# A hybrid decoder step on one core: the pooling copies go from ScalarE to VectorE, the last group's additions from GpSimd to VectorE, and the samples' last products are written later

## The chip, the cores and the metric

The kernel runs on one core of a Trainium2 chip. The metric is the device time of one execution in microseconds (us). A core has TensorE (matrix products, in the profile PE, with its weight loads as PEld), VectorE (DVE), ScalarE (ACT), GpSimd (POOL) and SyncE (SP), which here only issues transfers. Each engine works through its own queue in order.

## The reference

One layer of a decoder, for a prompt of 1024 rows and for 8 samples of 8 rows with their own states. All is float32.

```
h = rmsnorm(x) * (1 + scale) + shift                 # shift, scale, gate from silu(c) @ w_ada + b_ada
u_pool, z_pool, z_ssm, xBC, dt, g = split(h @ w_in)
P = (pool_mix(u_pool) * silu(z_pool)) @ w_pool_out   # pool_mix: means over 2, 4, 8, 16 rows, minus u,
                                                     # times pool_w (128x128 a group), times pool_scale
S = rmsnorm((SSD(silu(conv(xBC))) + D*x) * silu(z_ssm)) @ w_ssm_out
x = x + gate * ((sigmoid(g_pool) * P + sigmoid(g_ssm) * S) @ w_o)
y = rmsnorm(x)
```

It also returns the new states: the last 15 inputs of the pooling branch, the last 3 rows of the convolution's input, and the SSD state.

## The kernel before

Channels lie on the 128 partitions and the 1088 rows (1024 of the prompt, then 64 of the samples) along the free axis, up to the last product. Every large product is made of three TensorE products in a split format: each operand is halved into a high and a low part (`split`, L165 on ScalarE for the high part, L168 on GpSimd for the low one), and high x high, high x low and low x high are added in one PSUM bank. PSUM is handed out in pools: three banks named mm, four named ps, one named pc. Who asks for a bank waits until what was in it has been read.

The stages follow one another. First the norm and the modulation. Then `h @ w_in`, two blocks of 128 columns at a time, by a scheme of seven half-size products for eight (`pair`, `strassen`, `product`, L608 to L610); VectorE gathers the sums (L619, L624). Each pair's two column blocks have a generator for what happens to them afterwards: `u_unit` and `zp_unit` for the pooling branch (four pairs, with the windows 16, 8, 4 and 2 in this order), `conv_unit` for the convolution. Their steps are handed out between the products of later pairs (`between`, `step`). The last step of `u_unit`, the pooling tail, is what the first edit is about: the last 15 prompt rows and the sample rows of the group are turned by TensorE into one PSUM bank (L804, L805), copied out (L807, L808) and stored (L809, L810); then the means are multiplied by pool_w in three blocks of 256, 384 and 448 columns (L814), each copied out times pool_scale (L815). `zp_unit` multiplies that by silu(z) on VectorE (L828) and stores it.

Then comes the SSD in 4 groups of 8 chunks, with the products by w_pool_out (first) and w_ssm_out (three of the four groups of channels) woven in (L359 to L361, evicted by L1744). The fourth, last group stands by itself: for each of the 8 output tiles m, `tail_unit(m)` runs 36 products in three blocks, each added to the tile `acc[m]` from PSUM by VectorE (L1907); when the third is in, the tile is multiplied by the gate over the norm (L1912; the gate tile R is loaded by L1897 and scaled by L1900) and the pooling part m1 is added (L1913; loaded by L1902). For m = 0 to 6 the addition is GpSimd's, for m = 7, which goes in three blocks, VectorE's. Then `m_split` halves the tile for the last product: L1880 and L1881 for the samples' 64 columns, L1891 and L1892 for the prompt's 1024. Gate tiles have three buffers, so that the load for m + 3 waits for L1912 of m.

The last product, by w_o, turns the layout: for each of 8 blocks of 128 rows, two halves of 512 columns are summed over k = 0 to 7 (L2004 to L2006), times the gate (L2007), plus x, norm, store. The samples' rows have two sums of their own, over the same k, in a ps and the pc bank (`samples[k]`, L1886). Rows k = 0 to 4 of w_o (halves made earlier, loaded by `wo_prep`, L1873 and L1874) come early; rows 5 to 7 go to the buffers of the last group's inputs and can be loaded only when TensorE has read these. The function `sample_rows` finishes the samples between the blocks (L1968 and following).

SP's queue issues nearly all loads, in order; ScalarE's queue issues the stores. The order of the instructions on each engine isn't all written out by hand: the scheduler reorders within the traced program by a model of durations and by priorities, so an edit can shift instructions of other lines. In the SSD part TensorE and SP are held to the written order (`in_line`).

Of the kernel before, what the change touches and what calls it, by code (L numbers as in the profile page):

```python
# [10 lines left out]
AF = mybir.ActivationFunctionType  # L11
ALU = mybir.AluOpType
# [8 lines left out]
P = 128  # L21
# [4 lines left out]
NS = 64  # L26
# [20 lines left out]
def tile_pool_ssd_step(  # L47
# [6 lines left out]
    nc = tc.nc  # L54
    uid = [0]

    def nm(s):
        uid[0] += 1
        return f"{s}_{uid[0]}"
# [31 lines left out]
    def R(shape=(P, T), dt=F32):  # L91
        return hs.tile(list(shape), dt, tag="R", name=nm("R"), bufs=3)
# [4 lines left out]
    def PB():  # L97
        return psB.tile([P, 512], F32, tag="ps", name=nm("ps"))
# [14 lines left out]
    act = nc.scalar.activation  # L113
    V = nc.vector
# [31 lines left out]
    pscl = vT[:, 40:44]  # L146
# [601 lines left out]
    def GA(shape):  # L748
        return gas[0].tile(list(shape), F32, tag="GA", name=nm("GA"), bufs=7)

    def small(shape, tag, bufs):
        return gas[0].tile(list(shape), F32, tag=tag, name=nm(tag), bufs=bufs)
# [3 lines left out]
    def u_unit(gi):  # L756
        L = gi + 1
        stp = sm.tile([120, P], F32, tag="stc", name=nm("stp"), bufs=4)
        load(stp, state_pool[0, :, :, gi * P:(gi + 1) * P].rearrange("b t c -> (b t) c"))
        pwt = sm.tile([P, P], F32, tag="stc", name=nm("pwt"), bufs=4)  # L760
        load(pwt, pool_w[0, gi])
        yield
        up = GA([P, CW_])
        us = small([P, NB, 23], "us", 1)

        def done(o, n, comb, buf):
            e = min(o + n, SEQ) - o
            comb(up[:, 15 + o:15 + o + e], 0, e)
            if e < n:
                comb(us[:, :, 15:23], e, n, lambda t: t.rearrange("p (b t) -> p b t", t=8))  # L770
        yield done
        V.memset(up[:, 0:15], 0.0)
        ps = PB()
        nc.tensor.transpose(ps[:, :120], stp, ident[:120, :120])
        V.tensor_copy(us[:, :, 0:15], ps[:, :120].rearrange("p (b t) -> p b t", t=15))
        u64 = sm.tile([P, NB, 8], F32, tag="rsm", name=nm("u64"))
        act(u64, us[:, :, 15:23], AF.Copy)
        u15 = sm.tile([P, 27], F32, tag="t27", name=nm("u15"))
        act(u15[:, 0:15], up[:, SEQ:SEQ + 15], AF.Copy)
        yield  # L780
        a, av = up, us
        ab = [GA([P, T]) for _ in range(2)]
        for l in range(L):
            st = 1 << l
            o0 = 2 * st - 1
            b = ab[l % 2]
            bv = small([P, NB, 23], "bv", 2)
            V.tensor_tensor(b[:, o0:15 + SEQ], a[:, o0:15 + SEQ], a[:, o0 - st:15 + SEQ - st], ALU.add)
            V.tensor_tensor(bv[:, :, o0:], av[:, :, o0:], av[:, :, o0 - st:23 - st], ALU.add)
            a, av = b, bv  # L790
            if l or L < 4:
                yield 1
        wn = WINS[gi]
        d = ab[L % 2]
        V.scalar_tensor_tensor(d[:, :SEQ], a[:, 15:15 + SEQ], 1.0 / wn, up[:, 15:15 + SEQ], ALU.mult, ALU.subtract)
        e = sm.tile([P, 15], F32, tag="edge", name=nm("edge"), bufs=1)
        V.tensor_tensor(e[:, :wn - 1], a[:, 15:15 + wn - 1], rc[:, :wn - 1], ALU.mult)
        V.tensor_tensor(d[:, :wn - 1], e[:, :wn - 1], up[:, 15:15 + wn - 1], ALU.subtract)
        V.scalar_tensor_tensor(d[:, SEQ:].rearrange("p (b t) -> p b t", t=8), av[:, :, 15:], 1.0 / wn,
                               us[:, :, 15:], ALU.mult, ALU.subtract)  # L800
        yield 1
        yield 1
        ps = PB()
        nc.tensor.transpose(ps[:15, :P], u15[:, 0:15], ident)  # L804
        nc.tensor.transpose(ps[:NS, P:2 * P], u64.rearrange("p b t -> p (b t)"), ident)  # L805
        o15, o64 = [sm.tile([n, P], F32, tag="o27", name=nm("o15")) for n in (15, NS)]
        act(o15, ps[:15, :P], AF.Copy)  # L807
        act(o64, ps[:NS, P:2 * P], AF.Copy)  # L808
        store_(new_pool_p[0, 0, :, gi * P:(gi + 1) * P], o15)  # L809
        store_(new_pool_s[0, :, 7:15, gi * P:(gi + 1) * P], o64)  # L810
        y = up[:, :T]
        for o, n in BLK:
            ps = PB()
            mm(ps[:, :n], pwt, d[:, o:o + n], start=True, stop=True)  # L814
            act(y[:, o:o + n], ps[:, :n], AF.Copy, scale=pscl[:, gi:gi + 1])  # L815
        yp_[gi] = y
        yield 1

# [622 lines left out]
    def upair(gi):  # L1441
        return pair(C_UP + gi * P, C_ZP + gi * P, u_unit(gi), zp_unit(gi))
# [398 lines left out]
    def M(shape=(P, T), dt=F32):  # L1841
        return mq.tile(list(shape), dt, tag="m", name=nm("m"))
# [6 lines left out]
    ps = PB()  # L1849
    for c in range(9):  # L1850
        n = min(P, T - c * P)
# [5 lines left out]
    for c in range(9):  # L1857
        n = min(P, T - c * P)
# [7 lines left out]
    samples = []  # L1866

    def wo_prep(k, mem):
        if k < 4:
            hi, lo = w4[0][:, k, :D], w4[1][:, k, :D]  # L1870
        else:
            hi, lo = mem((P, D), F32R), mem((P, D), F32R)
        load(hi.bitcast(F32), wo_d[k][:, 0])  # L1873
        load(lo.bitcast(F32), wo_d[k][:, 1])  # L1874
        wo[k] = (hi, lo)

    def m_split(k, mem):

        sh = sm.tile([P, P], F32R, tag="stc", name=nm("sh"), bufs=4)
        act(sh[:, 0:NS], acc[k][:, SEQ:], AF.Copy)  # L1880
        V.tensor_tensor(sh[:, NS:P], acc[k][:, SEQ:], sh[:, 0:NS].bitcast(F32), ALU.subtract)  # L1881

        def sample_mm():
            for part in wo[k]:
                for half in range(2):
                    mm(pso[half], sh, part[:, half * 512:half * 512 + 512],  # L1886
                       start=(k == 0 and part is wo[k][0]), stop=(k == 7 and part is wo[k][1]))
        samples.append(sample_mm)
        hi, lo = mem((P, SEQ), F32R), mem((P, SEQ), F32R)
        for o, n in (((0, 384), (384, 384), (768, 256)) if k == 7 else ((0, SEQ),)):  # L1890
            act(hi[:, o:o + n], acc[k][:, o:o + n], AF.Copy)  # L1891
            V.tensor_tensor(lo[:, o:o + n], acc[k][:, o:o + n], hi[:, o:o + n].bitcast(F32), ALU.subtract)  # L1892
        mh[k], ml[k] = hi, lo

    def m_done(m):
        r = R()
        load(r, gs_d[m])  # L1897
        for j, ps in enumerate(rstd):
            s = slice(512 * j, min(512 * j + 512, T))
            V.tensor_tensor(r[:, s], ps[:, :s.stop - s.start], r[:, s], ALU.mult)  # L1900
        mt = M()
        load(mt, m1_d[m])  # L1902
        a = acc[m]

        def done(o, n, ps):
            s = slice(o, o + n)
            V.tensor_tensor(a[:, s], ps[:, :n], a[:, s], ALU.add)  # L1907
            if m < 7:
                s = slice(0, T)
                if o + n < T:  # L1910
                    return
            V.tensor_tensor(a[:, s], a[:, s], r[:, s], ALU.mult)  # L1912
            (nc.gpsimd if m < 7 else V).tensor_tensor(a[:, s], a[:, s], mt[:, s], ALU.add)  # L1913
        return done

    def tail_unit(m):
# [16 lines left out]

    def late(shape, dt=F32R):
        return slots.pop(0)[:, :shape[1]]
    for k in (5, 6):
        wo_prep(k, late)
        samples[k]()
    wo_prep(7, late)
    m_split(7, late)  # L1940
    sample_mm = samples[7]

    def w2k(tag):
        return wp.tile([P, 512], F32, tag=tag, name=nm("half"), bufs=4)
# [16 lines left out]
        nc.gpsimd.tensor_tensor(selS[:, pr], ident[:, 0:64], ident[:, 64:128], ALU.add)  # L1961

    def sample_rows():
        sample_mm()
        qs = []
        for half in range(2):
            q = w2k("wlo")
            act(q, pso[half], AF.Copy)  # L1968
            qs.append(q)
        yield  # L1970
        pq = PB()
        for half in range(2):
            mm(pq[64 * half:64 * half + 64, :], selS[:, 64 * half:64 * half + 64], qs[half], start=True, stop=True)
        V.tensor_tensor(gsm, pq, gsm, ALU.mult)
        V.tensor_tensor(gsm, gsm, xs_, ALU.add)
        act(xs_, gsm, AF.Square, accum_out=sso[:, 8:9])
        yield
        ps = PB()
        mm(ps[:, 0:1], selS, sso[:, 8:9], start=True, stop=True)
        act(sso[:, 8:9], ps[:, 0:1], AF.Sqrt, bias=eps, scale=1.0 / D)  # L1980
        V.reciprocal(sso[:, 8:9], sso[:, 8:9])
        V.scalar_tensor_tensor(gsm, gsm, sso[:, 8:9], fgs, ALU.mult, ALU.mult)
        for half in range(2):
            store_(ysr[:, half * 512:half * 512 + 512], gsm[64 * half:64 * half + 64])

    sample = sample_rows()
    for i in range(8):
        if i > 0:
# [10 lines left out]
        for j, (c0, cw) in enumerate(cuts):  # L1999
            s = slice(c0, c0 + cw)  # L2000
            ps = PB()
# [56 lines left out]
```

## Time and profile before

| | us |
|---|---|
| median of 3 runs | 1286.67 (1284.23 to 1289.22) |
| profiled execution, its own time | 1286.55 |
| its span in the profile | 1284.8 |
| TensorE busy | 1256.1 |
| VectorE busy | 897.6 |
| ScalarE busy | 662.2 |
| GpSimd busy | 670.9 |

The granted clock of TensorE was 0.998 of full speed on average. In a row of the waits view stand who waited for whom, the us in total, how often, and the longest. In a row of the timeline stand the start from the beginning of the span, the duration, engine, line, operation, tiles and shape, and in brackets how long the engine was idle before and what released it. PE durations are modelled and overlap: consecutive matmuls are told apart by their starts. "SPq" and "ACTq" are instructions of a queue that issue a transfer.

### The profile page before, as it was taken

Reading aid. Unit: us, or ns where it says so; the run is one execution under the profiler, and the core shown is the slowest. Engines: PE = TensorE matmul, PEld = TensorE weight load, DVE = VectorE, ACT = ScalarE, POOL = GpSimd, SP = SyncE. Lnnn points to the kernel's source line nnn. Section 1 sums busy time; section 2 is a strip of 40 time slices with the busy share of each in tenths; the row PEclk is TensorE's granted clock in tenths of the full one; section 3 lists DMA queues with packets and bytes.
Section 4 is the critical chain, followed back from the end, with each engine's and each line's share of the span. In section 5 each row is a group of like instructions: output and inputs, shape, how many; then the busy total and the mean of one; then the engine's idle time right before and its main releaser. Section 6 shows DMA issues by size and latency. Waiting matters only on the chain.

```text
span 1284.8 us, 26305 instructions
## 1 busy us (share of the span) xinstructions
PE 1256.1 (98%) x9739; PEld 1169.3 (91%) x9739; DVE 897.6 (70%) x1608; ACT 662.2 (52%) x1528; POOL 670.9 (52%) x563
## 2 busy tenths in 40 slices
PE   7999999999999999999999999999999999999997
PEld 6779999989999999999999999989888889999786
DVE  4686678965978688676676765587766877576443
ACT  4665347465556556454655554656675766202111
POOL 1007669678868878555444444355665867314000
PEclk9999999999999999999999999999999999999999
DMA  9736355465456544444556564999769898675631
GB/s 331 243 118 215 122 164 156 149 199 173 148 161 207 159 152 131 166 154 122 176 170 198 165 191 143 336 307 314 225 215 277 265 294 265 211 265 162 229 107 49
DMA packets 232769, 251.68 MB, mean 196 GB/s; under 512 B 29729, under 2 KB 176881, under 8 KB 232634
## 3 DMA queue, kind: packets, MB, share of 16 engines
q1 hardware_dynamic: 160544, 171.60, 42.9%
q10 hardware_dynamic: 72098, 78.41, 17.9%
q8 instruction: 77, 1.26, 0.4%
q14 instruction: 50, 0.41, 0.1%
HBM read 167.06 MB, written 83.01 MB: 195 GB/s over the span
## 4 chain that ended last, share of the span: by engine, by line
PE 63%; issue 7%; DMA 7%; POOL 4%; ACT 2%; DVE 2%; SPq 0%; ACTq 0%; POOLq 0%; DVEq 0%
PE ps L608 6%; PE ps L609 5%; PE ps L610 5%; PE mm L608 5%; PE mm L610 5%; PE mm L609 5%; PE mm L359 4%; PE mm L360 4%; PE mm L361 4%; PE ps L1213 3%; PE ps L2004 2%; PE ps L2006 2%; PE ps L2005 2%; PE pc L1535 2%; PE ps L1216 2%
## 5 line engine op out<-in xcount | busy, mean ns | idle before, releaser
L168 POOL TENSOR_TENSOR wlo<-rawA,whi 128x512 fp32r<-128x512 f32 x120 | 179.6, 1501 | 176.1 <-ACT whi L165 99.8
L168 POOL TENSOR_TENSOR wlo<-raw,whi 128x512 fp32r<-128x512 f32 x92 | 150.6, 1644 | 125.5 <-ACT whi L165 114.1
L359 PE MATMUL mm<-Y,whi 128*128 128x352 f32 (+1 forms) x480 | 163.5, 341 | 0.6 <-DVE G L1907 0.5
L360 PE MATMUL mm<-Y,whi 128*128 128x352 f32 (+1 forms) x480 | 157.4, 328 | 0.3 <-DVE Y L1573 0.3
L361 PE MATMUL mm<-Y,wlo 128*128 128x352 f32 (+1 forms) x480 | 156.8, 327 | 0.0
L608 PE MATMUL mm<-Y,whi 128*128 128x272 f32 x496 | 146.3, 295 | 0.6 <-DVE GA L624 0.5
L610 PE MATMUL mm<-Y,wlo 128*128 128x272 f32 x496 | 144.2, 291 | 2.2 <-POOL wlo L168 1.7
L608 PE MATMUL ps<-Y,whi 128*128 128x272 f32 x496 | 143.4, 289 | 2.5 <-ACT o L808 2.2
L609 PE MATMUL ps<-Y,whi 128*128 128x272 f32 x496 | 143.0, 288 | 0.0
L610 PE MATMUL ps<-Y,wlo 128*128 128x272 f32 x496 | 142.6, 287 | 0.0
L609 PE MATMUL mm<-Y,whi 128*128 128x272 f32 x496 | 142.6, 288 | 0.0
L1056 DVE SCALAR_TENSOR_TENSOR GA<-GA,cvT,GA 128x1112 f32<-128x1112 f32 x72 | 127.7, 1776 | 1.3 <-ACT GA L1053 1.3
L165 ACT ACTIVATE whi<-rawA 128x512 fp32r<-128x512 f32 x125 | 78.3, 627 | 89.7 <-PE ps L609 48.0
L165 ACT ACTIVATE whi<-raw 128x512 fp32r<-128x512 f32 x96 | 58.9, 627 | 104.6 <-DVE raw L554 48.7
L1201 ACT ACTIVATE dec<-dec,acT 128x128 f32<-128x128 f32 (+1 forms) x288 | 86.6, 383 | 23.2 <-POOL dec L1192 22.8
L610 PEld LDWEIGHTS mm<-Y,wlo 128*128 128x128 f32 x496 | 93.4, 188 | 3.8 <-POOL wlo L168 2.6
L359 PEld LDWEIGHTS mm<-Y,whi 128*128 128x128 f32 x480 | 90.2, 188 | 7.1 <-issue 4.8
L608 PEld LDWEIGHTS ps<-Y,whi 128*128 128x128 f32 x496 | 93.3, 188 | 3.1 <-ACT o L808 2.5
L608 PEld LDWEIGHTS mm<-Y,whi 128*128 128x128 f32 x496 | 93.3, 188 | 3.0 <-DVE GA L624 0.6
L609 PEld LDWEIGHTS mm<-Y,whi 128*128 128x128 f32 x496 | 93.4, 188 | 0.9
L610 PEld LDWEIGHTS ps<-Y,wlo 128*128 128x128 f32 x496 | 93.4, 188 | 0.0
L609 PEld LDWEIGHTS ps<-Y,whi 128*128 128x128 f32 x496 | 93.3, 188 | 0.0
(456 smaller groups left out, 3760.4 us busy)
## 6 DMA issues: line engine op xcount, KB each, us to landing
rawA<-in_w_in SPq DMA_DIRECT2D x46, 512.0 KB
dec<-acs_d SPq DMA_DIRECT2D x32, 512.0 KB
xbc<-GA ACTq DMA_DIRECT2D x24, 512.0 KB
rawA<-in_w_in SPq DMA_DIRECT2D x32, 256.0 KB
pw<-in_w_ssm_out ACTq DMA_DIRECT2D x32, 256.0 KB
ws<-ph ACTq DMA_DIRECT2D x32, 256.0 KB
ws<-pw SPq DMA_DIRECT2D x32, 256.0 KB
h<-in_state_ssm SPq DMA_DIRECT2D x32, 256.0 KB
```

The source lines that it names most:

```text
L165: ins = act(hi[:, :, :ncols], raw[:, :, :ncols], AF.Copy)
L168: (eng or nc.gpsimd).tensor_tensor(lo[:, :, :ncols], raw[:, :, :ncols], hi[:, :, :ncols].bitcast(F32), ALU.subtract)
L359: mm(ps[:, :n], a, rh[k][:, o:o + n], start=(k == 0), stop=False)
L360: mm(ps[:, :n], a, rl[k][:, o:o + n], start=False, stop=False)
L361: mm(ps[:, :n], b, rh[k][:, o:o + n], start=False, stop=(k == nk - 1))
L608: mm(p, hi, ah, start=(k == 0), stop=False)
L609: mm(p, hi, al, start=False, stop=False)
L610: mm(p, lo, ah, start=False, stop=(k == 3))
L1056: V.scalar_tensor_tensor(d[:, :n], rp[:, k:k + n], cvT[:, 24 * k + mc:24 * k + mc + 1], d[:, :n], ALU.mult, ALU.add)
L1201: act(dec[:, h], dec[:, h], AF.Exp, bias=acT[:S, c, 8 * g + h:8 * g + h + 1], scale=-1.0)
L1213: mm(o[hh], xd[:S, 2 * q + hh, :], dec[:S, 2 * q + hh], start=True, stop=state is None)
L1216: mm(o[hh], state[:, h * 64:h * 64 + 64], cE[:, h], start=False, stop=True)
```

## The change

Three edits. The pooling tail's five copies out of PSUM (L807, L808, three times L815) are made by VectorE; the scaled ones become `tensor_scalar` products. The addition L1913 is VectorE's for all eight tiles. And the samples' products with k = 5, 6, 7 (`samples[k]`) are traced not with the loads of w_o's last rows but at the start of `sample_rows`; `m_split(7)` is still where it was. The lines behind move up by two or three: L1946 becomes L1943, L2004 to L2007 become L2002 to L2005.

```diff
-        act(o15, ps[:15, :P], AF.Copy)
-        act(o64, ps[:NS, P:2 * P], AF.Copy)
+        V.tensor_copy(o15, ps[:15, :P])
+        V.tensor_copy(o64, ps[:NS, P:2 * P])
         store_(new_pool_p[0, 0, :, gi * P:(gi + 1) * P], o15)
         store_(new_pool_s[0, :, 7:15, gi * P:(gi + 1) * P], o64)
         y = up[:, :T]
         for o, n in BLK:
             ps = PB()
             mm(ps[:, :n], pwt, d[:, o:o + n], start=True, stop=True)
-            act(y[:, o:o + n], ps[:, :n], AF.Copy, scale=pscl[:, gi:gi + 1])
+            V.tensor_scalar(y[:, o:o + n], ps[:, :n], pscl[:, gi:gi + 1], None, ALU.mult)
...
             V.tensor_tensor(a[:, s], a[:, s], r[:, s], ALU.mult)
-            (nc.gpsimd if m < 7 else V).tensor_tensor(a[:, s], a[:, s], mt[:, s], ALU.add)
+            V.tensor_tensor(a[:, s], a[:, s], mt[:, s], ALU.add)
...
-    for k in (5, 6):
+    for k in (5, 6, 7):
         wo_prep(k, late)
-        samples[k]()
-    wo_prep(7, late)
     m_split(7, late)
-    sample_mm = samples[7]
...
     def sample_rows():
-        sample_mm()
+        for k in (5, 6, 7):
+            samples[k]()
         qs = []
```

In the built order, the instructions move as follows. VectorE: the five copies stand behind the L624 that precede the tail's step (in two of the four groups the third scaled copy behind one more L624); L1913 stands one to five instructions behind the L1912 of its tile. TensorE: around each pooling tail the products of one bank change places with those of another, and the samples' products shift by some places. SP: two loads of x_prompt (L1991) stand ahead of w_o's last rows, and final_g's load (L1946) behind them. No instruction is added or dropped but for these moves.

## The prediction

> **What bounds the kernel now.** I read the page first, then TensorE's row of the waits view, then the busy time by stretch, and last the timeline of the places that the change touches. The page:
>
> ```profile
> span 1284.8 us, 26305 instructions
> ...
> PE 1256.1 (98%) x9739; PEld 1169.3 (91%) x9739; DVE 897.6 (70%) x1608; ACT 662.2 (52%) x1528; POOL 670.9 (52%) x563
> ```
>
> TensorE is busy 1256.1 of 1284.8 us, so all that any regrouping of the other engines can give back is 28.7 us, and only where it ends a stand of TensorE. The change removes no matmul. So the question is which stands of TensorE end on an instruction that the change moves. The waits view of the whole span, TensorE's rows that touch the change:
>
> ```profile
> PE ps L608 <- ACT o L808: 2.2, 1, 2.2
> ...
> PE mm L359 <- DVE G L1907: 0.5, 1, 0.5
> ...
> PE ps L1886 <- DMA Y<-wo: 0.3, 2, 0.2
> ```
>
> Columns are us in total, times, longest. The first is a copy that the change moves; the second is the eviction of the last group, done by the engine that gets the additions; the third is a sample product waiting for w_o's rows, which the last edit moves. Busy time of two stretches (TensorE, weight loads, VectorE, ScalarE, GpSimd):
>
> ```profile
> 258.00:270.00 12.00, 9.52 (x65) 8.39 (x64) 1.73 (x4) 9.37 (x23) 8.07 (x7) 1.00 0.44 136
> ...
> 1140.00:1194.00 54.00, 53.36 (x296) 49.62 (x295) 42.12 (x69) 9.95 (x18) 21.07 (x9) 1.00 0.58 190
> ```
>
> In the first, around the second pooling tail, TensorE loses 2.48 us while ScalarE is the full engine (9.37 of 12) and VectorE is empty (1.73). In the second, the last group, TensorE loses only 0.64 and VectorE has 11.9 us free. The granted clock is 1.00 in both.
>
> **Edit 1, the pooling copies.** The timeline of TensorE, ScalarE and VectorE there:
>
> ```profile
> 258.03 0.27 PE L805 MATMUL ps<-ident,u 128*64 128x128 f32 x1
> ...
> 261.89 0.91 PE L814 MATMUL ps<-GA,pwt 128*128 128x448 f32 x2
> ...
> 263.14 0.29 PE L608 MATMUL mm<-Y,whi 128*128 128x272 f32 x1
> 265.66 0.39 PE L608 MATMUL ps<-Y,whi 128*128 128x272 f32 x1 [2.23 <-ACT o L808]
> ```
>
> ```profile
> 262.68 1.30 ACT L1053 ACTIVATE GA<-GA,cvT 128x1112 f32<-128x1112 f32 x1
> ...
> 265.36 0.25 ACT L808 ACTIVATE o<-ps 64x128 f32<-64x128 f32 x1
> ```
>
> ```profile
> 258.23 0.42 DVE L624 TENSOR_TENSOR GA<-u,ps 128x272 f32<-128x272 f32 x1
> ...
> 268.98 1.29 DVE L828 TENSOR_TENSOR GA<-GA,GA 128x1088 f32<-128x1088 f32 x1 [6.05 <-ACT GA L815]
> ```
>
> The transposes (L804, L805) are done at 258.3. Their PSUM bank is emptied by L807 and L808, which stand in ScalarE's queue behind the convolution's L1053, and only run at 265.4. TensorE needs that bank, the fourth of four, at 263.3 and stands 2.23 us. VectorE meanwhile has nothing to do: it too waits for ScalarE (6.05 us before L828). Prices of such copies on VectorE, from the start of the kernel, by shape, and what the scaled copies cost ScalarE today:
>
> ```profile
> L241 DVE COPY tf<-ps 128x448 f32<-128x448 f32 x4 | 2.5, 622 | 5.3 <-PE ps L233 5.1
> ...
> L241 DVE COPY tf<-ps 128x384 f32<-128x384 f32 x4 | 2.2, 551 | 0.4 <-PE ps L233 0.4
> ...
> L241 DVE COPY tf<-ps 128x256 f32<-128x256 f32 x4 | 1.7, 422 | 1.9 <-PE ps L233 1.9
> ...
> L775 DVE COPY us<-ps 128x120 f32<-128x120 f32 x4 | 1.1, 269 | 0.0
> ```
>
> ```profile
> L815 ACT ACTIVATE GA<-ps,vT x12: 445/558/635, 170.7 to 479.9; 128x256 f32<-128x256 f32 x4, 128x384 f32<-128x384 f32 x4, 128x448 f32<-128x448 f32 x4
> ```
>
> No row shows a scaled copy from PSUM on VectorE; I price it as the plain copy of its shape. One group then costs VectorE 2 x 0.27 + 0.42 + 0.55 + 0.62 = 2.13 us, four groups 8.5 us, about what ScalarE gives up. In the second group VectorE is free at 258.65 (258.23 + 0.42), has the two small copies out at 259.19, the next two at 260.16, and the third, whose product ends at 261.89 + 0.91 = 262.80, at 263.42. The bank is free 4 us before TensorE asks for it, so the 2.23 us go. What is queued behind the third copy is a memset that waited for a TensorE transpose anyway, and the product L828, which now runs at 263.4 and not at 268.98. The stores L809 and L810 stay on ScalarE's queue and wait for VectorE, but the copies are out before ScalarE gets there. The other three groups show no TensorE stand on these copies: nothing there.
>
> For the price from above I take the worst stretch that VectorE shows beside GpSimd. Both rows are of the last group, the second while GpSimd's addition ran:
>
> ```profile
> 1141.16 1.28 DVE L1912 TENSOR_TENSOR G<-G,R 128x1088 f32<-128x1088 f32 x1
> ...
> 1143.36 2.85 DVE L1912 TENSOR_TENSOR G<-G,R 128x1088 f32<-128x1088 f32 x1
> ```
>
> ```profile
> 1142.52 2.55 POOL L1913 TENSOR_TENSOR G<-G,m 128x1088 f32<-128x1088 f32 x1 [32.55 <-DVE G L1912]
> ```
>
> A stretch of 1.57 us on each small copy puts the bank free at 258.65 + 2 x 1.84 = 262.3, still before 263.3. So edit 1 gives between 1.5 us (part of the stand comes back at a next bank) and 2.4 us; I take 2.2. [...]
>
> **Edit 2, the additions of the last group.** Seven additions leave GpSimd, at:
>
> ```profile
> L1913 POOL TENSOR_TENSOR G<-G,m x7: 2527/2548/3462, 1142.5 to 1182.9; 128x1088 f32<-128x1088 f32 x7
> ```
>
> VectorE does one in 1.28 us (L1912 alone, same shape), 8.96 us in all, and the stretch of 1.57 goes. VectorE's load in the 54 us becomes 42.12 + 8.96 - 1.57 = 49.5. What hides it are VectorE's own stands there:
>
> ```profile
> DVE R L1900 <- DMA R<-gs: 6.4, 3, 2.4
> DVE sh L1881 <- ACT sh L1880: 4.4, 3, 2.2
> ```
>
> A gate tile for output tile m+3 can be fetched once L1912 of tile m has read its buffer, and VectorE stands for it three times; with the addition in its queue just there, it comes later to a tile that lands when it did. The stands behind L1880 shrink too: L1880 follows the addition, which takes 1.28 and not 2.5 to 3.5 us. So the L1907 that TensorE's banks wait for comes no later than now, and the chain addition, split, half is shorter. The one stand on L1907:
>
> ```profile
> 1163.17 0.32 PE L360 MATMUL mm<-Y,whi 128*128 128x352 f32 x1
> 1163.34 0.32 PE L361 MATMUL mm<-Y,wlo 128*128 128x352 f32 x1
> 1164.20 0.44 PE L359 MATMUL mm<-Y,whi 128*128 128x384 f32 x1 [0.55 <-DVE G L1907]
> ```
>
> By starts it is 0.86 where the pace is 0.17: 0.69 us. That L1907 stood behind L1900 and L1892; the order built for the changed kernel puts it among the L1900 of the same tile. I count 0.69 as gone; from the other side the same sort of stand can recur at each of seven tiles, priced below.
>
> **Edit 3, samples' products later.** In the built order of TensorE the twelve products of k = 5, 6, 7 stand two places later than before; their number and the last eviction behind them are the same: nothing by itself. What changes is SP's queue: final_g's load now stands behind w_o's last rows, and two loads of x_prompt stand ahead of them.
>
> ```profile
> 1187.87 1.22 DVE L1892 TENSOR_TENSOR G<-G,G 128x1024 fp32r<-128x1024 f32 x1
> ```
>
> ```profile
> 1189.15 0.36 SPq L1946 DMA_DIRECT2D G<-in_final_g  x1
> 1189.61 0.37 SPq L1873 DMA_DIRECT2D Y<-wo  x1
> ```
>
> ```profile
> 1186.37 0.32 PE L361 MATMUL mm<-Y,wlo 128*128 128x352 f32 x1
> ...
> 1194.21 0.39 PE L2006 MATMUL ps<-m,G 128*128 128x512 f32 x1
> 1194.76 0.47 PE L1886 MATMUL ps<-Y,sh 128*128 128x512 f32 x1 [0.16 <-DMA Y<-wo]
> ...
> 1195.30 0.84 PE L2004 MATMUL ps<-Y,G 128*128 128x512 f32 x3
> 1196.32 0.51 PE L1886 MATMUL ps<-Y,sh 128*128 128x512 f32 x1 [0.18 <-DMA Y<-wo]
> ```
>
> The buffer for w_o's rows is free when the last group's last product is read (1186.7). The load went out at 1189.61, because final_g's load ahead of it waited for L1892 (over at 1189.09). With the second x_prompt load waiting only for the addition of tile 6, now early, w_o's rows go out up to 2.9 us sooner. TensorE stood 0.55 - 0.23 = 0.32 and 1196.32 - 1195.30 - 3 x 0.23 = 0.33 us for them (pace (0.84 - 0.39)/2 = 0.23): 0.65 us go. Cover is 2.9 against 0.65; if the x_prompt load is late, the 0.65 stay.
>
> **The sum.** 2.2 + 0.69 + 0.65 = 3.5 us. The profiled execution took 1286.55 us (span 1284.8, 1.75 around it), 0.1 below the median of 1286.67. Forecast 1286.55 - 3.5 = 1283.0. A measurement of this kernel can tell about 0.5% (6.4 us) from no change, so this is no change.
>
> **Rivals.**
> *The last group becomes VectorE's.* If its stands stay (6.4 + 4.4 = 10.8, because each gate tile's fetch waits for a product that the added work delays), 49.5 + 10.8 = 60.3 us are wanted of 54, and without the relief of 1.57 it is 61.9: 6.3 to 7.9 us on TensorE's banks. That makes 1286.55 + 6.3 to 7.9 = 1292.9 to 1294.5 if the pooling gain gets lost in it, and 2.2 less (from 1290.7) if not. It decides where L1912 of tile m ends later than now. For it: VectorE is at 78% there already. Against it: the stands are just where the additions go. [...] 20%, of which 14% beyond 0.5%.
> *The early lead is lost.* The 2.2 us are won at 263; 860 us later another queue may set the pace, and only the last group's 1.3 us stay: 1285.2. Against it: TensorE stands for so little in between. 15%.
> *More goes than these stands.* TensorE's waits from 282 to 1127 us for the three engines whose queues shift:
>
> ```profile
> PE mm L610 <- POOL wlo L168: 1.9, 4, 0.8
> ...
> PE ps L1512 <- DVE cE L1530: 1.1, 1, 1.1
> PE ps L1326 <- ACT s L651: 0.8, 2, 0.4
> ```
>
> They sum to 3.8; ScalarE, 8.5 us lighter, feeds GpSimd's halves. All gone: 1283.0 - 3.8 = 1279.2. 13%.
> *The forecast* 52%.
>
> **How the numbers follow.** Faster by over 0.5% needs under 1280.1: the third rival, 0.13. Slower by over 0.5% needs over 1293.0: 0.14 from the first. The rest, 0.73, is within. The range reaches down to the third rival's 1279.2, and up into the first's 1290.7 to 1294.5, where it leaves out what is worst: 1279.0 to 1292.0. The likeliest case alone runs from 1282.0 (2.4 and 2.1, starts counted everywhere) to 1285.0.
>
> **What would show it.** Right: no TensorE wait on L808 or L807 near 263; L828 directly behind VectorE's third scaled copy; the scaled copies at 0.42, 0.55 and 0.62; L1912 at 1.28 in every tile; VectorE near 49 us busy in the last group; no wait on w_o's rows. Wrong: TensorE waiting on L1907 more than once, VectorE's wait for gate tiles still at 6 us, or another wait of about 2 us behind 263.

## Result, and the profile after

The changed kernel takes 1283.01 us (median of 7 runs, 1280.71 to 1284.38) against 1287.11 for the kernel before (7 runs, 1284.23 to 1289.22). The ratio is 0.9964, 95% interval [0.9951, 0.9977]: 3.0 to 6.3 us less. Forecast were 1283.0 us and a difference within 0.5%; both hold. Measured twice more beside the kernel before, the ratio was 0.9964 and 0.9963; one execution of 5911 us, far above all others, is left out of the first of these. The total is right, but several of the steps behind it are not.

The profiled execution of the changed kernel took 1284.38 us, 1.4 above its median. Its page:

```profile
span 1282.6 us, 26320 instructions
...
PE 1256.3 (98%) x9739; PEld 1170.9 (91%) x9739; DVE 911.9 (71%) x1635; ACT 654.9 (51%) x1508; POOL 653.9 (51%) x556
```

VectorE gained 14.3 us, ScalarE lost 7.3 and GpSimd 17.0; TensorE's work is what it was. The span fell by 2.2 us only, so the profile has to be read by place. A row with x2 merges two instructions, from the start of the first to the end of the last. First the second pooling tail, as VectorE did it:

```profile
257.76 0.42 DVE L624 TENSOR_TENSOR GA<-u,ps 128x272 f32<-128x272 f32 x1
258.10 0.27 DVE L807 COPY o<-ps 15x128 f32<-15x128 f32 x1
258.31 0.27 DVE L808 COPY o<-ps 64x128 f32<-64x128 f32 x1
258.50 0.99 DVE L815 TENSOR_SCALAR GA<-ps,vT 128x256 f32<-128x256 f32 x2
262.37 0.68 DVE L815 TENSOR_SCALAR GA<-ps,vT 128x448 f32<-128x448 f32 x1 [2.88 <-PE ps L814]
263.01 0.06 DVE L1036 MEMSET GA<- 128x3 f32 x1
263.09 1.41 DVE L828 TENSOR_TENSOR GA<-GA,GA 128x1088 f32<-128x1088 f32 x1
```

The bank of the transposes is free at 258.6, four us before TensorE asks for it; no wait on L807 or L808 is left, and L828 runs at 263.09 instead of 268.98. But TensorE's waits from 262 to 300 us hold one that before did not have; the second row shows it in the timeline:

```profile
PE mm L610 <- POOL wlo L168: 1.4, 1, 1.4
```

```profile
280.01 0.39 PE L610 MATMUL mm<-Y,wlo 128*128 128x272 f32 x1 [1.41 <-POOL wlo L168]
```

Busy time around the tail, just behind it, at the start of the last stage, and in the last group (TensorE, weight loads, VectorE, ScalarE, GpSimd, then the granted clock):

```profile
258.00:270.00 12.00, 11.63 (x85) 10.75 (x84) 7.43 (x13) 9.21 (x22) 10.32 (x8) 1.00 0.46 133
270.00:282.00 12.00, 10.59 (x85) 10.37 (x84) 11.91 (x17) 5.06 (x11) 7.89 (x4) 1.00 0.62 216
1126.00:1130.00 4.00, 4.00 (x21) 3.97 (x21) 1.45 (x7) 0.41 (x2) 0.00 (x0) 0.76 0.92 311
1130.00:1134.00 4.00, 4.00 (x24) 4.00 (x24) 1.72 (x7) 0.00 (x0) 0.00 (x0) 0.81 0.98 346
1138.00:1192.00 54.00, 54.00 (x305) 51.08 (x304) 48.35 (x80) 9.97 (x18) 0.60 (x2) 1.00 0.65 220
```

TensorE loses 0.37 us in the first stretch where it lost 2.48, but 1.41 in the second. The last group is closed: 54.00 of 54.00, with VectorE at 48.35.

How far TensorE is ahead of the kernel before, from the starts of the same product (counted by the columns done so far) in the two profiles:

| up to | ahead by (us) | what lies between |
|---|---|---|
| 249 | 0.59 | small differences since the start |
| 272 | 2.95 | the stand on L808 is gone: +2.36 |
| 291 | 1.28 | the new wait on L168: -1.67 |
| 400 | 1.56 | two transposes (L1038) near 374 stand side by side: +0.29 |
| 769 | 0.42 | several small ones: -1.14 |
| 996 | 1.68 | before stood 1.29 at 993 (L1512 on L1530), after not: +1.26 |
| 1155 | 0.13 | lower clock in after, 1126 to 1134: -1.55 |
| 1183 | 1.36 | the stands on L1907 are gone: +1.23 |
| 1217 to the end | 2.23 | the waits for w_o's rows are gone: +0.87 |

The rows at 996 and at 1155 touch nothing that was edited, and the experiments show that both come and go (for the first, with a doubt told under "Before, once more"). The small ones between 400 and 769 vary too: over this stretch the lead moves by -1.1, +0.2 and -0.2 in the three profiles of the changed kernel. The +0.29 does not vary. It is the order of TensorE's products, which the change shifted. Before:

```profile
374.18 0.24 PE L1038 MATMUL ps<-ident,stc 24*128 24x24 f32 x1
...
375.05 0.24 PE L1038 MATMUL ps<-ident,stc 24*128 24x24 f32 x1
```

After:

```profile
372.91 0.30 PE L1038 MATMUL ps<-ident,stc 24*128 24x24 f32 x2
```

In all nine profiles with the scaled copies on VectorE the two stand side by side and the lead grows by 0.29 to 0.30 here; in the five with these copies on ScalarE they stand apart and it doesn't. So five rows are the change's: 2.36 - 1.67 + 0.29 + 1.23 + 0.87 = 3.1.

### The profile page after: what moved, and what is told of

Its sections match the earlier page's. It is cut to its first block, busy times and chain, and to the rows that moved or that the text cites. A ratio compares the mean times of both kernels' runs of the same rounds, so it can differ in the third digit from the quotient of the medians.

```text
span 1282.6 us, 26320 instructions
## 1 busy us (share of the span) xinstructions
PE 1256.3 (98%) x9739; PEld 1170.9 (91%) x9739; DVE 911.9 (71%) x1635; ACT 654.9 (51%) x1508; POOL 653.9 (51%) x556
## 3 DMA queue, kind: packets, MB, share of 16 engines
q8 instruction: 77, 1.26, 0.4%
## 4 chain that ended last, share of the span: by engine, by line
PE 74%; issue 3%; DMA 2%; DVE 2%; POOL 2%; ACT 1%; ACTq 0%; SPq 0%; POOLq 0%; DVEq 0%
PE mm L359 7%; PE mm L360 6%; PE mm L361 6%; PE ps L608 6%; PE ps L609 6%; PE mm L608 6%; PE ps L610 6%; PE mm L610 6%; PE mm L609 6%; PE ps L1213 3%; PE ps L2002 2%; PE ps L2003 2%; PE ps L2004 2%; PE pc L1535 2%; PE ps L1216 2%
## 5 line engine op out<-in xcount | busy, mean ns | idle before, releaser
L168 POOL TENSOR_TENSOR wlo<-rawA,whi 128x512 fp32r<-128x512 f32 x120 | 180.3, 1506 | 169.5 <-ACT whi L165 90.1
L168 POOL TENSOR_TENSOR wlo<-raw,whi 128x512 fp32r<-128x512 f32 x92 | 148.7, 1623 | 124.0 <-ACT whi L165 111.2
L610 PE MATMUL mm<-Y,wlo 128*128 128x272 f32 x496 | 144.2, 291 | 4.5 <-POOL wlo L168 4.0
L610 PE MATMUL ps<-Y,wlo 128*128 128x272 f32 x496 | 142.6, 287 | 0.0
L1056 DVE SCALAR_TENSOR_TENSOR GA<-GA,cvT,GA 128x1112 f32<-128x1112 f32 x72 | 125.5, 1746 | 1.9 <-ACT GA L1053 1.8
L610 PEld LDWEIGHTS mm<-Y,wlo 128*128 128x128 f32 x496 | 93.4, 188 | 6.5 <-POOL wlo L168 5.4
L610 PEld LDWEIGHTS ps<-Y,wlo 128*128 128x128 f32 x496 | 93.4, 188 | 0.0
```

The source lines that it names most:

```text
L168: (eng or nc.gpsimd).tensor_tensor(lo[:, :, :ncols], raw[:, :, :ncols], hi[:, :, :ncols].bitcast(F32), ALU.subtract)
L610: mm(p, lo, ah, start=False, stop=(k == 3))
L1056: V.scalar_tensor_tensor(d[:, :n], rp[:, k:k + n], cvT[:, 24 * k + mc:24 * k + mc + 1], d[:, :n], ALU.mult, ALU.add)
```

## Experiments

Theory A for the new wait came from ScalarE's queue. These are its rows in the changed kernel, with SP's store L441, which it waits for:

```profile
267.00 0.39 ACTq L829 DMA_DIRECT2D yp<-GA  x1
...
274.71 0.39 ACTq L426 DMA_DIRECT2D pw<-in_w_ssm_out  x1
275.20 0.64 ACT L435 ACTIVATE ph<-pw 128x512 fp32r<-128x512 f32 x1 [5.65 <-DMA ws<-pw]
```

```profile
266.99 0.38 SPq L540 DMA_DIRECT2D rawA<-in_w_in  x1
...
268.25 10.38 SPq L441 DMA_DIRECT2D ws<-pw  x2
```

Besides the input's weights, the kernel halves the later weights a piece at a time: load L426, high half L435 on ScalarE, low half L437 on GpSimd, stores. Two buffers (pw) take turns, so L426 must wait until the store L441 of its buffer has landed, and everything behind it on ScalarE waits too (L435 for 5.65 us). In the changed kernel L441 goes out at 268.25 and L426 at 274.71, 6.46 later; before, at 269.10 and 272.32, 3.22 later. What stands ahead of L441 in the changed kernel is the product's store L829 (0.56 MB), at 267.00; before it came at 270.31, behind L441. GpSimd then does L437 and L168 late:

```profile
275.92 2.37 POOL L437 TENSOR_TENSOR pw<-pw,ph 128x512 fp32r<-128x512 f32 x1 [4.11 <-ACT ph L435]
278.25 4.04 POOL L168 TENSOR_TENSOR wlo<-rawA,whi 128x512 fp32r<-128x512 f32 x2
```

The readings of all 14 profiles side by side; before_again, after_again and after_third are the two kernels unaltered, and the runs named e are explained below. "Stand" is a step between starts over its usual pace; "gap" is from the issue of L441 to that of L426; "dip" is what the products of the 7 us behind L1852 (1121 to 1133, by kernel) lose over their pace.

| profile | stand near 263 | gap | stand near 278 | stand on L1907 near 1162 | stand near 992 | dip |
|---|---|---|---|---|---|---|
| before | 2.40 (L808) | 3.22 | none | 0.71 | 1.29 | 0.19 |
| before_again | 2.34 (L808) | 3.30 | none | 0.67 | 1.00 | 1.67 |
| e2_add | 2.27 (L808) | 3.14 | none | none | none | 1.65 |
| e3_late | 2.19 (L808) | 3.23 | none | 0.71 | none | 1.71 |
| after | none | 6.46 | 1.58 | none | none | 1.70 |
| after_again | none | 6.05 | 0.71 | none | 0.73 | 1.59 |
| after_third | none | 5.86 | 0.55 | none | none | 1.70 |
| e1_pool | none | 6.57 | 1.56 | 0.67 | none | 0.19 |
| e6_double | none | 5.64 | 0.31 | none | none | 0.19 |
| e4_yplater | none | 4.45 | none | none | 0.23 | 1.67 |
| e4_again | none | 4.01 | none | none | none | 0.19 |
| e4_third | none | 4.54 | none | none | none | 1.66 |
| e5_small | 1.66 (L815) | 3.49 | none | none | none | 0.19 |
| e7_pwsp | none | L426 is SP's | none | none | 0.85 | 1.72 |

**The three edits, each alone.** Each kernel is the changed one with the other two edits undone, by the diff shown with the change.

> Edit 1 alone; last group and tail as before. Theory A (2.2 us won at the second pooling tail, 1.7 of it taken back 15 us later when a longer store of a split weight holds ScalarE's queue and GpSimd's weight half comes late): no TensorE wait on L808 near 263, VectorE's scaled copies at 0.42/0.55/0.62, a TensorE wait on L168 of 1.2 to 1.8 us near 278, the stands on L1907 (0.5) and on w_o's rows (0.3) as before; 0.5 to 1.3 us under before, about 1286.2. Rival B (the 278 stand of the changed kernel's profile was chance): L808 gone, nothing above 0.6 us at 278, 2.2 to 2.6 us under before, about 1284.7. Rival C (the pooling copies give nothing at the end): within 0.3 us of before.

Measured: ratio 0.9977 [0.9967, 0.9986], 1284.15 us against 1287.6: 1.8 to 4.2 us less. The stand on L808 is gone and the one near 278 is there in its full size, so rival B falls on the trace and C on the time; the time itself is below what A expected, by more than the trace of this run explains by edit 1.

> Edit 2 alone: the seven additions on VectorE, pooling copies on ScalarE, sample products where they were. Theory (the added 9 us lie in VectorE's own stands): VectorE 48 to 50 us busy in the 54 us of the last group, L1912 at 1.28 in all tiles, no TensorE wait on L1907, the stand on L808 (2.2) still there at 263; 0.7 to 1.3 us under before, about 1286.1. With w_o's rows sooner as well (the second x_prompt load no longer waits for a late addition), up to 1.9 under. Rival (the last group becomes VectorE's): several TensorE waits on L1907, 2 to 8 us over before.

Measured: 0.9982 [0.9973, 0.9990], 1.3 to 3.5 us less, no TensorE wait at all from 1138 to 1200. In the trace both gains of the tail are there, 1.25 us up to 1183 and 0.84 up to 1217. So the sooner rows of w_o come with edit 2 alone, as the expectation had it as its second possibility. SP's queue shows it, in e2_add and then in e3_late:

```profile
1184.63 0.33 SPq L1873 DMA_DIRECT2D Y<-wo  x1
...
1187.78 0.39 SPq L1946 DMA_DIRECT2D G<-in_final_g  x1
```

> Edit 3 alone: the twelve sample products of k = 5, 6, 7 two places later, additions still on GpSimd. In the order built for it SP's loads in the tail stand as before (final_g ahead of w_o's rows), so by the prediction's step the sooner rows need edit 2 as well. Theory: w_o's rows at the same place, the stands on them (0.3 us) stay or shrink because their products come later; 0 to 0.65 us under before, 1286.5 to 1287.1. Rival (the later place costs): the last eviction comes later, 0.3 to 1 us over before.

```profile
1188.28 0.36 SPq L1943 DMA_DIRECT2D G<-in_final_g  x1
1188.74 0.38 SPq L1873 DMA_DIRECT2D Y<-wo  x1
```

Measured: 1.0003 [0.9994, 1.0011]. Edit 3 does nothing by itself that the time shows, and the ratios of the three edits alone multiply to 0.9962, close to the 0.9964 of all three. final_g's load is ahead of w_o's rows as before, and TensorE waits 0.3 us for them at another product; its waits from 1138 to 1200:

```profile
PE mm L359 <- DVE G L1907: 0.5, 1, 0.5
PE ps L2002 <- DMA Y<-wo: 0.3, 1, 0.3
```

**The product's store, later.** The edit holds the store of this one group back until the next piece of the later weights has been halved (lines behind 436 move by 6: L835 is L829, L447 is L441, L616 is L610, L443 is L437):

```diff
-        store_(yp_d[:, gi], sz)
+        pend.append(lambda: store_(yp_d[:, gi], sz)) if gi == 2 else store_(yp_d[:, gi], sz)
...
                 store_(jobs[n][2][:, 0], hi.bitcast(F32))
+            if 0 < len(pend) < 3:
+                pend.append(None)
+            elif pend:
+                with behind(mybir.EngineType.Activation):
+                    pend.pop(0)()
+                pend.clear()
```

> The changed kernel with one difference: the 0.56 MB store of the second pooling group's product (L829, at 267 in the profile) stands seven places later on ScalarE's queue, behind the load of a split weight (L426) that waits for the store of its buffer (L441); every other queue is in the changed kernel's order. Theory A (the early product store shares the DMA engines with that store and so lengthens it): L426 goes out at 273.2 +- 0.5 and not at 274.7, GpSimd's half L168 is 1.2 to 1.6 us sooner, the TensorE wait at 278 falls from 1.58 to under 0.5, 1.0 to 1.5 us under the changed kernel: about 1281.8. Rival B (the store takes as long behind the 0.5 MB input load alone): L426 still at 274.2 or later, the wait at 278 still 1.2 us or more, time that of the changed kernel, 1283.0.

> The changed kernel unaltered, beside the next two on one chip. Theory A: the TensorE wait on L168 near 278 recurs with 1.4 to 1.7 us, L426 again goes out 6 to 7 us after the store that it waits for; the stand on L1530 near 993 of the first profile of before is absent again, and the lower granted clock of 1126 to 1134 may or may not be there (0.57 to 1.00 in five profiles so far): 1282 to 1284. Rival (the stand at 278 was chance): it is under 0.6 us this time.

> The kernel with the later product store once more, on the chip of the unaltered changed kernel: its trace has no wait at 278; what is open is whether the time follows. Theory A: 1.0 to 1.5 us (0.08 to 0.12%) under the changed kernel of the same call. Rival (the lead is lost again further on, at the next pooling group or later): 0 +- 0.4 us, with another stand of about 1 us more between 300 and 1200 than in the changed kernel's trace.

> The changed kernel unaltered, for the time beside the next one: ratio to before 0.9955 to 0.9975 (0.9964 twice so far). Trace: L426 6.0 to 6.6 us behind the split weight's store, a stand of 0.7 to 1.6 us on L168 near 278.

> The changed kernel with the later product store (L829 behind L426), for the time beside the unaltered one on one chip. Theory A: no stand near 278, L426 4.0 to 4.5 us behind the store, 0.7 to 1.8 us under the changed kernel, ratio to before 0.994 to 0.996. Rival (the lead of 278 is lost further on): the same time to 0.4 us.

ScalarE's and SP's rows of the second profile with the later store (e4_again):

```profile
271.87 0.38 ACTq L426 DMA_DIRECT2D pw<-in_w_ssm_out  x1
272.35 0.63 ACT L435 ACTIVATE ph<-pw 128x512 fp32r<-128x512 f32 x1 [3.35 <-DMA ws<-pw]
...
273.50 0.33 ACTq L835 DMA_DIRECT2D yp<-GA  x1
```

```profile
266.60 0.38 SPq L546 DMA_DIRECT2D rawA<-in_w_in  x1
...
267.86 7.04 SPq L447 DMA_DIRECT2D ws<-pw  x2
```

```profile
270.00:282.00 12.00, 12.00 (x97) 11.75 (x96) 10.82 (x14) 7.57 (x19) 8.89 (x7) 1.00 0.83 270
```

With the store out of the way the gap is 4.01 to 4.54 us in three profiles, and TensorE is busy 12.00 of 12.00 us behind the tail in each; with the store ahead it is 5.64 to 6.57 in five. The stand near 278 exists in all five profiles of the early store (0.31 to 1.58) and in none of the three of the late one. That the early store lengthens the gap, and that the lead goes there, is shown; for what the two transfers compete isn't. The expectations for the changed kernel were a little high: after_again has 0.71 where 1.4 to 1.7 were expected, after_third 0.55 and a gap of 5.86 where at least 0.7 and 6.0 were.

The size of the stand varies with something more: in after and e1_pool, GpSimd's L437 took 2.37 and 2.28 us, in after_again, after_third and e6_double 1.29 to 1.30, and that 1 us is the difference between the stands of 1.6 and those of 0.7 or less. The traces point to who starts first. In after, VectorE's L1056 started at 275.75 and L437 at 275.92; in after_third L437 was first:

```profile
275.75 1.37 DVE L1056 SCALAR_TENSOR_TENSOR GA<-GA,cvT,GA 128x1112 f32<-128x1112 f32 x1
```

```profile
273.79 1.29 POOL L437 TENSOR_TENSOR pw<-pw,ph 128x512 fp32r<-128x512 f32 x1 [3.52 <-ACT ph L435]
```

```profile
274.22 2.03 DVE L1056 SCALAR_TENSOR_TENSOR GA<-GA,cvT,GA 128x1112 f32<-128x1112 f32 x1
```

Whichever came second was the longer one. Of all 14 profiles, this L437 takes 2.28 to 2.37 us in the eight where L1056 was already running at its start, and 1.28 to 1.48 in the other six. So a gap that is 0.4 us longer can cost 1 us more, by bringing L437 behind L1056. This is read from the order in the traces; no run changed that order alone.

In time: 1280.72 against 1281.6 us on one chip, 1279.9 against 1280.95 on another. The ratios to before are 0.9960 [0.9946, 0.9973], 0.9949 [0.9936, 0.9962] and 0.9957 [0.9944, 0.9970] with the later store, 0.9964, 0.9964 and 0.9963 without. The later store was ahead three times of three, by about 1 us in the two direct comparisons, the size of the stand removed, but each pair's intervals overlap: the best version so far on all medians, not shown to be faster than the changed kernel by its time alone.

**The load off ScalarE's queue.**

```diff
-                store_(raws[n], jobs[n][0].rearrange("(k p) c -> p k c", p=P))
+                load(raws[n], jobs[n][0].rearrange("(k p) c -> p k c", p=P))
```

> The changed kernel with the loads of the split weights (L426) issued by SP instead of ScalarE, so that it is SP's queue and not ScalarE's that stands until their buffer's store has landed. Theory A (a wait in ScalarE's in-order queue holds what lies behind it): ScalarE's idle gaps of 5.6 us at 269.5 and 6.5 us at 511 shrink below 2 us, the waits on L168 (4.4 us in total in the changed kernel) fall below 2, 1 to 3 us under the changed kernel. Rival (SP's queue takes the stand and brings the input loads late): waits of GpSimd, ScalarE or VectorE on rawA grow, and TensorE waits on L165 or L554 appear, 2 us or more over the changed kernel.

Measured: 0.9969 [0.9958, 0.9980], 1282.29 us beside 1281.6: no gain. Half of the expectation holds. At 270.67 ScalarE goes straight on to L435 and the stand near 278 is gone (a smaller one, 0.42 us on L168, stands at 269). At 511 its gap has not shrunk: ScalarE now waits just as long for the piece itself, which SP loads later:

```profile
515.95 1.28 ACT L434 ACTIVATE pw<-pw,vT 128x128 f32<-128x128 f32 x4 [6.67 <-DMA pw<-in_w_ssm_out]
```

TensorE's waits on L168 sum to 3.7 us (2.5 in after_again), with one of 1.25 at 552, larger than any there in the changed kernel. So the wait for the store was passed on to another queue; it was not removed.

**The small copies only.**

```diff
-            V.tensor_scalar(y[:, o:o + n], ps[:, :n], pscl[:, gi:gi + 1], None, ALU.mult)
+            act(y[:, o:o + n], ps[:, :n], AF.Copy, scale=pscl[:, gi:gi + 1])
```

> The changed kernel with the three scaled copies (L815) back on ScalarE: of edit 1 only the two small copies (L807, L808) are VectorE's; edits 2 and 3 stay. Theory A (the stand at 263 is the small copies' alone, and what is lost at 278 comes from the earlier product store): no wait on L808; the product store goes out 2 to 3 us later than in the changed kernel, behind the split weight's store or less than 1 us ahead of it; L426 follows that store by under 5 us (6.0 to 6.6 with the early store, 4.0 to 4.5 with the late one); no wait over 0.5 us at 278: 1.0 to 1.8 us under the changed kernel, 0.9945 to 0.9955 of before. Rival (the scaled copies on ScalarE keep PSUM banks as long): a TensorE wait on L815 of 0.5 to 2 us near 263, time that of the changed kernel or up to 1 us over it.

Measured: 0.9982 [0.9972, 0.9992]. The product's store is late again (268.44, behind L441 at 267.21), the gap is 3.49 and nothing stands near 278: so far A. But the next bank of the four now waits for ScalarE:

```profile
265.35 0.39 PE L608 MATMUL ps<-Y,whi 128*128 128x272 f32 x1 [1.50 <-ACT GA L815]
```

1.66 us of the 2.4 come back, and the expected time is missed: the rival holds for this half. By the ratios the time is 2.3 us over the changed kernel, where the rival allowed 1; the intervals overlap. The scaled copies have to move with the small ones.

**The added VectorE work, doubled.** Behind each of the seven additions a second instruction of the same size, an unneeded subtraction into m1's buffer:

```diff
             V.tensor_tensor(a[:, s], a[:, s], mt[:, s], ALU.add)
+            if m < 7:
+                V.tensor_tensor(mt[:, s], a[:, s], mt[:, s], ALU.subtract)
```

> The changed kernel with a second VectorE instruction of the same size behind each of the seven additions of the last group (an unneeded subtraction that writes m1's buffer, read by nothing behind it): the added work of edit 2 twice. Theory (the addition lies in VectorE's stands, which are used up by now: 48.35 us of 54 are busy): 48.35 + 7 x 1.28 = 57.3 us wanted of 54, TensorE waits on L1907 in several tiles, 2.5 to 5 us over the changed kernel. Rival (the order in VectorE's queue matters and not the load, the stands for gate tiles had room for twice as much): within 0.6 us of the changed kernel, at most one wait on L1907.

```profile
1138.00:1192.00 54.00, 54.00 (x296) 50.23 (x295) 52.17 (x78) 9.97 (x18) 0.60 (x2) 1.00 0.70 229
1140.00:1180.00 40.00, 40.00 (x234) 38.49 (x233) 40.00 (x59) 7.23 (x12) 0.60 (x2) 1.00 0.62 193
1180.00:1200.00 20.00, 20.00 (x88) 16.18 (x87) 13.07 (x22) 3.81 (x8) 0.00 (x0) 1.00 0.77 288
```

Measured: 0.9969 [0.9956, 0.9982], 1281.95 us: the time of the changed kernel. VectorE is busy 40.00 of 40.00 us and TensorE never waits for it. The instructions are there (L1915, 7 of 1.28 us); what the stage cannot take is done later: VectorE has 13.07 us from 1180 to 1200 where the changed kernel has 8.59. The theory of the experiment fails. Its rival has the time and the waits right, but not its reason that the stands had room for twice as much: the load did fill the engine. The evictions that TensorE needs (L1907) stand in VectorE's queue between the long instructions and came in time, so a full VectorE was late only with what nobody waits for.

**Before, once more.**

> The kernel before, unaltered, one look. Theory: the stand on L808 (2.0 to 2.3 us at 262 to 263) and the one on L1907 (0.7 near 1162) recur; L426 follows the split weight's store by 3.2 to 3.5 us with no wait of 0.5 us or more near 278; the stand on L1530 near 993 (1.29 us in the first profile of before, 0 to 0.85 in the profiles of the others) and the lower clock of 1126 to 1134 come and go and belong to neither kernel. If the stand of 1.29 recurs in full, it may belong to the kernel before, and part of the gain with it.

It was as expected: 2.34 and 0.67 us on L808 and L1907, gap 3.30. The stand on L1530 is 1.00 here; after_again and e7_pwsp have 0.73 and 0.85, e4_yplater 0.23, the nine others under 0.1, e3_late among them, whose order there is that of before. The clock dipped this time and not the first (1.67 against 0.19 us lost). The dip belongs to no kernel; of the stand near 992 that is less sure, since before had it both times and the others in 3 of 12 profiles, and smaller.

## Why the prediction was right, and where not

**Edit 1, 2.2 us at 263: right where it was priced.** The stand measured 2.40 by starts and is gone in all profiles with the whole edit; the lead grows by 2.36. L828 stands directly behind the third scaled copy (but for a memset). "The other three groups [...] nothing there" was 0.29 short: the changed order near 374, at the third tail, gives that much without any wait that a view would show. The copies cost a little more than priced, 0.46, 0.60 and 0.68 against 0.42, 0.55 and 0.62:

```profile
L815 DVE TENSOR_SCALAR GA<-ps,vT 128x448 f32<-128x448 f32 x4 | 2.7, 684 | 6.4 <-PE ps L814 6.4
L815 DVE TENSOR_SCALAR GA<-ps,vT 128x384 f32<-128x384 f32 x4 | 2.4, 602 | 0.1
L815 DVE TENSOR_SCALAR GA<-ps,vT 128x256 f32<-128x256 f32 x4 | 1.9, 463 | 0.0
```

**The step that failed:** "the product L828, which now runs at 263.4 and not at 268.98", told as a harmless consequence. L828 has a store behind it, L829, which comes forward with it, past SP's store L441, and this was not followed. It cost 0.4 to 1.7 us of lead in the five profiles that have the early store, 1.67 in the one of after. "Another wait of about 2 us behind 263" was named as a sign of error, and it came. The rival of the lost early lead (15%) thus held in part, but with the wrong place and mechanism: lost 15 us later, not in some queue 860 us on.

**Edit 2, 0.69 us: right in sign, too small.** VectorE's load was forecast at 49.5 us of 54. In the fixed window from 1138 to 1192 it is 48.35, 46.56 and 45.27 in the three profiles of the changed kernel, but that window holds different work in each. Between the same two products that the 54 us of before lie between, it is 46.6 in all three, and these now take 52.75 us. The forecast took off only the 1.57 of one L1912; the eight L1881 in this stretch also fell, from 478 to 218 ns on average. L1912 is at 1.28 us in all seven tiles that it takes whole (at most 1289 ns), where before one of them took 2.85 beside GpSimd's addition: with the additions on VectorE no stretched L1912 is left. VectorE's waits in the last group shrank as argued:

```profile
DVE R L1900 <- DMA R<-gs: 1.4, 2, 1.1
...
DVE sh L1881 <- ACT sh L1880: 0.3, 1, 0.3
```

That is 1.7 us where there were 10.8. The term was short because a second stand on L1907, of 0.25 us at 1156, and the slower first product behind each of the two (0.10 and 0.11 over the pace) were not counted: 0.71 + 0.25 + 0.21 = 1.17, measured 1.23 and, alone, 1.25.

**"The last group becomes VectorE's" (20%): it did not come, and no run shows the mechanism that priced it.** It held that load over the stage's time comes out as waits of TensorE. In e6_double, VectorE is full for 40 us and there is not one wait, with 46.6 + 7 x 1.28 = 55.6 us wanted of 52.75. The rival's 60.3 of 54 were reached in no run, since the stands that it kept did not stay (1.7 us of 10.8). The rival put 1290.7 to 1294.5 into the range; without it the range would have ended near 1285.

**Edit 3, 0.65 us: the gain came (0.87), but it isn't edit 3's.** The step said "what changes is SP's queue" under edit 3. e3_late has SP's old order and the old wait, e2_add has the new order and none. The order belongs to the additions, the only thing that e2_add changes; why the scheduler then puts w_o's rows ahead of final_g's load was not followed. 0.65 was short by the same slower product behind a stand (0.11 at 1196), and by another 0.1 that I can't place.

**The sum.** 3.5 forecast; 2.36 - 1.67 + 0.29 + 1.23 + 0.87 = 3.1 by this profile, 3.0 to 6.3 by the times. From the base of 1286.55 the 3.1 give 1283.5. With the 0.81 and 0.65 us of lead that after_again and after_third lose at 278, in place of 1.67, the same sum is 3.9 and 4.1 (an estimate); the medians lie 4.1 apart. The hit of 1283.0 has luck in it: 1.67 us missed at 278 were partly made up by terms that were 0.9 too small in sum (0.16, 0.54 and 0.22) and by the 0.29 that were not counted, and the rest lies within what a single base profile can tell, which here had 1.29 us of the stand near 992 and no dip of the clock.

## What to carry to other kernels

When an edit lets an instruction run sooner, follow its store or load too, and ask which transfer it now overtakes and which in-order queue stands waiting for that one: here a store that came 3.3 us sooner cost up to 1.67 us of lead. VectorE, busy 40.00 of 40.00 us in e6_double, did not make TensorE wait once: before pricing a full engine's load as a loss, ask where in its queue the instructions sit that others need. And when a gain is well under the spread of single profiles, compare stands place by place in several of them, since a clock change (here 1.59 to 1.72 us lost, against 0.19) or a stand of another line (1.29) can be as large as the edit.

## What the hardware showed that was not expected

After a store of 256 KB was issued, the next load of its buffer went out 4.0 to 4.5 us later where the store was 1.26 us behind a 512 KB load, and 5.6 to 6.6 where a further store of 544 KB was ahead of it. Where it came 2.3 to 2.6 us behind the load, it was landed when ScalarE got there, 3.1 to 3.5 us later.

TensorE's granted clock drops behind eighteen products of one column (L1852) in 9 of 14 profiles, of both kernels; there the following products lose 1.59 to 1.72 us, in the other five 0.19, with nothing between. In the profile of after:

```profile
1124.66 2.05 PE L1852 MATMUL ps<-ones,sq_acc 128*128 128x1 f32 x18
...
1127.95 0.40 PE L360 MATMUL mm<-Y,whi 128*128 128x384 f32 x1
1128.14 0.52 PE L361 MATMUL mm<-Y,wlo 128*128 128x384 f32 x1
1128.46 0.52 PE L359 MATMUL mm<-Y,whi 128*128 128x384 f32 x1
...
1131.18 0.47 PE L359 MATMUL mm<-Y,whi 128*128 128x352 f32 x1
1131.48 0.34 PE L360 MATMUL mm<-Y,whi 128*128 128x352 f32 x1
```

From 1128.14 to 1131.48 the starts are 0.29 to 0.33 us apart, where they are 0.16 to 0.19 outside: about half speed for some 3.3 us. From 1126 to 1130 the granted clock is 0.76 here, 0.57 to 0.95 in the nine profiles with the drop and 1.00 in the five without. What brings the drop about is not shown by any run: it stands behind the 2.05 us of one-column products each time it comes, and the same products run without it in the other five. These 1.5 us alone are as large as most of what the edits moved.
